# The first two weight groups of a stage as one pair: context products of all four tiles, then the latent ones

## Chip, cores and metric

The kernel runs on one core of a Trainium2 chip. The metric is device time in microseconds of one execution, as the median of several. The time before is 1759.61 us, the median of 3 runs (1754.5 to 1765.26).

## What is computed

Two layers of a backbone over 256 latent and 256 context tokens with 1024 channels. The context tokens use the same weights. Of the second layer only the latent output is wanted, but its scans start from the context's final state, so its mixer still projects the context.

```python
for l in range(DEPTH):                       # DEPTH = 2
    need_ctx = l < DEPTH - 1
    ...
    hl = rms_norm(xl, g_pre_mix[l]) * (1.0 + ml[1]) + ml[0]
    hc = rms_norm(xc, g_pre_mix[l]) * (1.0 + mc[1]) + mc[0]
    yc, yl = mixer(hc, hl, lp, lb_all[l], rows, need_ctx)
    xl = xl + ml[2] * rms_norm(yl, g_post_mix[l])
    hl = rms_norm(xl, g_pre_ffn[l]) * (1.0 + ml[4]) + ml[3]
    xl = xl + ml[5] * rms_norm(conv_ffn(hl, ffn_w_up[l], ...), g_post_ffn[l])
    if need_ctx:
        ...                                  # the same for xc
```

The mixer begins with `z = h @ w_in` (the first 1024 columns feed a depthwise convolution and the recurrent gates), the feed-forward stage with `u = h @ w_up`, whose 2 x 2816 columns are a gate half with a convolution and a value half that is multiplied by it.

## The kernel before

**Columns.** The activations stand as columns: `h` is a pair of tiles `hi` and `lo`, for each of eight k (128 channels each) with the latent tokens in columns 0 to 255 and the context tokens in 256 to 511. In a mixer a third block of 256 columns holds the latent tokens in column-major order, copied there by `columns_order` (L457 to L462, eight copies of `hi` and eight of `lo` on ScalarE).

**Products.** All large products run in split form. A weight group of 1024 x 256 is loaded by one transfer (`prep`, L247 to L251, tile `raw`), cut into two tiles of 128 columns, and each is split in `piece` (L224 to L238) into `whi` (ScalarE, L236) and `wlo` (VectorE, L237). `mm3` (L240 to L244) issues three products for each k: `whi` with `hi` (L242), `whi` with `lo` (L243), `wlo` with `hi` (L244). A tile over all eight k is 24 products, into one PSUM bank of the four named `mm`. `feat_group` (L253 to L263) does this for the two tiles of a group, over a list of views: one view is a slice of PSUM columns and of `h`.

**The split view.** Where a stage's `h` becomes ready in two parts, its first groups use two views, first the context columns 256 to 511, then the latent ones. A tile is then 24 context products and 24 latent products of 256 columns. That is so for the first two groups of layer two's mixer (the string PAT, L680, with `split` for n < 2), and for the first gate group and the first value group of the first layer's feed-forward stage (`ffn`, L1103 to L1109).

**What comes ahead of them.** The sub-layer before ends in `post` (from L473): for the context rows first and then the latent rows, ScalarE squares (L481), VectorE scales by the gate (L482) and adds the residual (L485), the row is squared again (L427) and scaled (L430), TensorE transposes it (L444, tiles `ax`), ScalarE writes `hi` (L449), VectorE writes `hf` (L451) and `lo` (L453). The context's `h` is so ready some time ahead of the latent one.

**What sets the order.** The program is recorded in the order of the code; a scheduler then places each instruction on its engine by priority and by when its tiles can have memory. `post` is recorded with a priority offset of 3000 and the splitting of weights with one of 300. Each engine runs its list in that order. Pieces come from the pool `wp` with three buffers of `whi` and of `wlo`; `raw` has three buffers too. A pool opened for a stage (`rg` in the mixer, `fw` in the feed-forward stage) lies where the pool `xp` of the rows lay before, and its tiles wait for the last use of what was there. Between the groups `aside` (L266) issues steps of the next conditioning vectors, whose additions are L306 and L308 on VectorE.

**After the second place.** The evacuation of a tile of the first 1024 columns is `conv` (ScalarE L555, VectorE L559). With two tiles done, `recur` issues eight gate products (L605), whose results ScalarE turns into sigmoids (L93) after a table load.

```python
    def feat_group(self, w, c0, views, evac, pieces=None):
        narrow = all(sl.stop - sl.start < 512 for sl, _ in views)
        pieces = pieces or self.prep(w, c0, line=int(narrow))
        for mt, (hi, lo) in enumerate(pieces):
            ps = self.psum()
            for sl, mv in views:
                for k in range(KD):
                    self.mm3(ps[:, sl], (hi[:, k, :], lo[:, k, :]), mv(k), k == 0, k == KD - 1)
            evac(c0 // P + mt, ps)
        self.aside()
```

Of the kernel before, what the change touches and what calls it, by code (L numbers as in the profile page):

```python
# [14 lines left out]
P = 128  # L15
D = 1024
KD = D // P
S = 256
DEPTH = 2
DFF = 2816  # L20
# [11 lines left out]
PAT = ['XFRXFRXFRXFFRFFF', 'XXRXFRXFRFFFRFFF']  # L32
# [19 lines left out]
class Net:  # L52
# [200 lines left out]
# [7 lines that stand above are left out]
                for k in range(KD):  # L260
                    self.mm3(ps[:, sl], (hi[:, k, :], lo[:, k, :]), mv(k), k == 0, k == KD - 1)
            evac(c0 // P + mt, ps)
        self.aside()  # L263


# [268 lines left out]
    def rg_phase(self, l, h, need_ctx, dr, first, more):  # L534
        nc, tc, I = self.nc, self.tc, self.ins
        C = self.cols[l]
        w_in = I["w_in"][l]
# [6 lines left out]
        with tc.tile_pool(name=self.nm("rg"), bufs=1, reuse_waits="tile") as pool:  # L544
# [106 lines left out]
            rgx = [(O_RGX + g * 256, conv) for g in range(4)]  # L651

            split = [(slice(S, 512), lambda k: (h[0][:, k, S:512], h[1][:, k, S:512])), lat[0]]
# [12 lines left out]
            def groups(lst, n, view):  # L666
                for _ in range(n):
                    c0, ev = lst.pop(0)
                    if c0 is None:
                        spill_v(ev)  # L670
                        continue
                    if first:
                        for mt, ps in enumerate(first.pop(0)):
                            ev(c0 // P + mt, ps)
                        continue
                    self.feat_group(w_in, c0, view, ev)

            gate_w(0), gate_w(1)
            b = 0
            for n, c in enumerate(PAT[l]):  # L680
                if c == "R":
                    recur((2 * b, 2 * b + 1))
                    b += 1
                    if b == 1:
                        self.columns_order(h)
                    if b < 4:
                        gate_w(2 * b), gate_w(2 * b + 1)
                elif c == "X":
                    groups(rgx, 1, split if n < 2 else both)
                else:  # L690
                    groups(fill, 1, main if need_ctx and n > 1 or not need_ctx else split)
# [376 lines left out]
    def ffn(self, l, h, need_ctx, ffp, pool):  # L1068
# [3 lines left out]
        w = I["ffn_w_up"][l]  # L1072
        view = [(slice(0, W), lambda k: (h[0][:, k, 0:W], h[1][:, k, 0:W]))]
# [26 lines left out]
                nc.scalar.activation(out=fh[st][t], in_=fs, func=AF.Copy)  # L1100
                nc.vector.tensor_tensor(out=fl[st][t], in0=fs, in1=fh[st][t], op=ALU.subtract)

        split = view  # L1103
        if need_ctx:
            split = [(slice(S, 512), lambda k: (h[0][:, k, S:512], h[1][:, k, S:512])),
                     (slice(0, S), lambda k: (h[0][:, k, 0:S], h[1][:, k, 0:S]))]
        for g in range(KF // 2):
            self.feat_group(w, g * 256, view if g else split, gpart)
            self.feat_group(w, DFF + g * 256, view if g else split, vpart)  # L1109
        return fh, fl  # L1110

    def run(self):
# [169 lines left out]
```

## Time and profile before

| what | value |
|---|---|
| median of 3 runs | 1759.61 us (1754.5 to 1765.26) |
| the profiled execution, its own time | 1755.87 us |
| its span | 1754.1 us |
| TensorE busy in the span | 1678.9 us, 96% |
| VectorE, ScalarE, GpSimd busy | 1269.9, 903.1, 39.6 us |
| mean granted clock of TensorE | 0.993 |
| moved by DMA | 282.91 MB, mean 161 GB/s |

The span runs from the first to the last instruction of the profiled execution. Busy shares are means over stages with different limits. A row of the timeline gives start, duration, engine, line, operation, what it writes and reads, how many were merged, and in square brackets how long the engine stood idle before it and which instruction released it. Products overlap, so their durations are longer than their distance. Some product records are missing from a trace.

### The profile page before, as it was taken

Reading aid. Unit: us, or ns where it says so; the run is one execution under the profiler, and the core shown is the slowest. Engines: PE = TensorE matmul, PEld = TensorE weight load, DVE = VectorE, ACT = ScalarE, POOL = GpSimd, SP = SyncE. Lnnn points to the kernel's source line nnn. Section 1 sums busy time; section 2 is a strip of 40 time slices with the busy share of each in tenths; the row PEclk is TensorE's granted clock in tenths of the full one; section 3 lists DMA queues with packets and bytes.
Section 4 is the critical chain, followed back from the end, with each engine's and each line's share of the span. In section 5 each row is a group of like instructions: output and inputs, shape, how many; then the busy total and the mean of one; then the engine's idle time right before and its main releaser. Section 6 shows DMA issues by size and latency. Waiting matters only on the chain.

```text
span 1754.1 us, 30468 instructions
## 1 busy us (share of the span) xinstructions
PE 1678.9 (96%) x12243; PEld 1411.8 (80%) x12243; DVE 1269.9 (72%) x2305; ACT 903.1 (51%) x1563; POOL 39.6 (2%) x65
## 2 busy tenths in 40 slices
PE   5999999999999999999999999999999999979998
PEld 3777888888888787878878877778997778969996
DVE  3788777788697787997776466777557777767764
ACT  4887723344444445533333355888445555556543
POOL 1000000000000000000000000000000000000000
PEclk9999999999999999999999999999999999989999
DMA  9422376332333377445554575332873224555663
GB/s 299 134 84 85 125 230 220 121 121 98 98 123 100 108 252 267 149 162 195 182 194 141 192 267 194 103 96 91 268 241 126 85 85 133 161 189 193 194 226 120
DMA packets 234201, 282.91 MB, mean 161 GB/s; under 512 B 16028, under 2 KB 210236, under 8 KB 234060
## 3 DMA queue, kind: packets, MB, share of 16 engines
q1 hardware_dynamic: 231068, 271.35, 46.9%
q10 hardware_dynamic: 2880, 9.51, 1.6%
q8 instruction: 96, 1.57, 0.4%
q14 instruction: 45, 0.37, 0.1%
q0 software_dynamic: 112, 0.11, 0.0%
HBM read 263.09 MB, written 17.85 MB: 160 GB/s over the span
## 4 chain that ended last, share of the span: by engine, by line
PE 71%; DVE 14%; ACT 6%; DMA 5%; issue 2%; POOL 1%; SPq 1%; POOLq 0%; DVEq 0%; ACTq 0%
PE mm L242 17%; PE mm L243 17%; PE mm L244 17%; DVE wlo L237 3%; PE mm L514 3%; PE mm L513 3%; PE mm L516 3%; DMA raw<-in_w_ada_dram 2%; DVE acc L308 2%; ACT whi L236 2%; PE ax L858 1%; ACT r L93 1%; PE ax L514 1%; PE ax L516 1%; POOL rs L418 1%
## 5 line engine op out<-in xcount | busy, mean ns | idle before, releaser
L242 PE MATMUL mm<-hi,whi 128*128 128x512 f32 (+1 forms) x1792 | 617.9, 346 | 1.5 <-ACT whi L236 1.0
L243 PE MATMUL mm<-lo,whi 128*128 128x512 f32 (+1 forms) x1792 | 615.0, 343 | 4.3 <-DVE lo L453 4.2
L237 DVE TENSOR_TENSOR wlo<-raw,whi 128x1024 fp32r<-128x1024 f32 (+1 forms) x408 | 436.2, 1080 | 249.0 <-ACT whi L236 236.1
L244 PE MATMUL mm<-hi,wlo 128*128 128x512 f32 (+1 forms) x1792 | 613.8, 343 | 2.1 <-DVE wlo L237 2.0
L236 ACT ACTIVATE whi<-raw 128x1024 fp32r<-128x1024 f32 (+1 forms) x408 | 378.8, 944 | 444.0 <-PE mm L243 223.1
L242 PEld LDWEIGHTS mm<-hi,whi 128*128 128x128 f32 x1792 | 337.4, 189 | 46.9 <-issue 4.3
L243 PEld LDWEIGHTS mm<-lo,whi 128*128 128x128 f32 x1792 | 337.5, 188 | 45.2 <-DVE lo L453 5.6
L244 PEld LDWEIGHTS mm<-hi,wlo 128*128 128x128 f32 x1792 | 336.8, 188 | 43.0 <-DVE wlo L237 3.1
L308 DVE SCALAR_TENSOR_TENSOR acc<-raw,s,acc 128x256 f32<-128x256 f32 x448 | 192.7, 478 | 1.8
L873 DVE TENSOR_TENSOR QK<-QK,T 128x512 f32<-128x512 f32 (+1 forms) x84 | 101.6, 1220 | 9.6 <-PE ax L858 6.3
L243 PE MATMUL mm<-wlo,hi 128*128 128x256 f32 x256 | 71.4, 279 | 3.1 <-DVE wlo L237 3.1
L242 PE MATMUL mm<-whi,hi 128*128 128x256 f32 x256 | 72.1, 282 | 1.1 <-ACT whi L236 0.9
L882 ACT ACTIVATE kt<-QK 128x256 f32<-128x256 f32 (+1 forms) x60 | 40.9, 690 | 58.8 <-DVE QK L873 38.3
L244 PE MATMUL mm<-whi,lo 128*128 128x256 f32 x256 | 71.2, 278 | 0.0
L514 PE MATMUL mm<-wlo,fh 128*128 128x512 f32 x176 | 68.5, 389 | 0.0
L513 PE MATMUL mm<-whi,fh 128*128 128x512 f32 x176 | 68.5, 389 | 0.0
L418 POOL TENSOR_TENSOR rs<-ms,mhalf 128x1 f32<-128x1 f32 (+2 forms) x42 | 29.4, 701 | 1535.4 <-DVE ms L416 1535.4
L516 PE MATMUL mm<-whi,fl 128*128 128x512 f32 x176 | 54.2, 389 | 0.0
L243 PEld LDWEIGHTS mm<-wlo,hi 128*128 128x128 f32 x256 | 48.1, 188 | 3.8 <-DVE wlo L237 3.5
L242 PEld LDWEIGHTS mm<-whi,hi 128*128 128x128 f32 x256 | 48.2, 188 | 3.0 <-ACT whi L236 1.1
L93 ACT ACTIVATE acc<-acc 128x512 f32<-128x512 f32 (+1 forms) x44 | 22.6, 515 | 53.9 <-DVE acc L1089 53.9
L244 PEld LDWEIGHTS mm<-whi,lo 128*128 128x128 f32 x256 | 48.3, 189 | 0.0
(225 smaller groups left out, 2456.3 us busy)
## 6 DMA issues: line engine op xcount, KB each, us to landing
raw<-in_w_in_dram SPq DMA_DIRECT2D x72, 1024.0 KB
raw<-in_w_ada_dram SPq DMA_DIRECT2D x48, 1024.0 KB
raw<-in_ffn_w_up_dram SPq DMA_DIRECT2D x44, 1024.0 KB
raw<-in_ffn_w_down_dram SPq DMA_DIRECT2D x33, 1024.0 KB
raw<-in_w_out_dram SPq DMA_DIRECT2D x12, 1024.0 KB
raw<-in_w_proj_rg_dram SPq DMA_DIRECT2D x8, 1024.0 KB
raw<-in_w_proj_hg_dram SPq DMA_DIRECT2D x8, 1024.0 KB
xs<-xt SPq DMA_DIRECT2D x10, 512.0 KB
```

The lines of the kernel that those rows point to most:

```text
L236: nc.scalar.activation(out=v(hi)[:, part, :], in_=src[:, part, :], func=AF.Copy)
L237: nc.vector.tensor_tensor(out=v(lo)[:, part, :], in0=src[:, part, :], in1=v(hi)[:, part, :], op=ALU.subtract)
L242: nc.tensor.matmul(out=out, lhsT=L[0], rhs=R[0], start=start, stop=False)
L243: nc.tensor.matmul(out=out, lhsT=L[0], rhs=R[1], start=False, stop=False)
L244: nc.tensor.matmul(out=out, lhsT=L[1], rhs=R[0], start=False, stop=stop)
L308: nc.vector.scalar_tensor_tensor(out=at, in0=r3[:, k, :], scalar=s, in1=at, op0=ALU.mult, op1=ALU.add)
L418: nc.gpsimd.tensor_tensor(out=rs, in0=ms, in1=self.mhalf[:, 0:n], op=ALU.pow)
L513: nc.tensor.matmul(out=out, lhsT=ah, rhs=hi[:, n, :], start=k == 0, stop=False)
L514: nc.tensor.matmul(out=out, lhsT=ah, rhs=lo[:, n, :], start=False, stop=False)
L516: nc.tensor.matmul(out=pss[i][n], lhsT=al, rhs=hi[:, n, :], start=False, stop=k == nk - 1)
L873: nc.vector.tensor_tensor(out=u, in0=u, in1=sub(t, 1, [[-1, 2], [2, W2 // B], [0, B]]), op=ALU.mult)
L882: nc.scalar.activation(out=kt.rearrange("p (n h j) -> p n h j", h=2, j=B), in_=sub(qk, W2, [[2 * B, W2 // (2 * B)], [W2 + B, 2], [1, B]]), ...
```

## The change

A new function `feat_pair` takes two groups. It splits the first group's tiles into the pool `wp` as before and the second group's tiles into the pool of the stage, takes four PSUM banks, issues the context products of all four tiles, then the latent products of all four, then the four evacuations. It replaces the first two groups of layer two's mixer, and the first gate and value group of the first layer's feed-forward stage.

```diff
+    def feat_pair(self, parts, views, pool):
+        jobs = []
+        for j, (w, c0, evac) in enumerate(parts):
+            for mt, p in enumerate(self.prep(w, c0, (pool, pool) if j else (None, None), 1)):
+                jobs.append((c0 // P + mt, p, evac, self.psum()))
+        for sl, mv in views:
+            for _, (hi, lo), _, ps in jobs:
+                for k in range(KD):
+                    self.mm3(ps[:, sl], (hi[:, k, :], lo[:, k, :]), mv(k), k == 0, k == KD - 1)
+        for m, _, evac, ps in jobs:
+            evac(m, ps)
+        self.aside()
+        self.aside()
...
-            for n, c in enumerate(PAT[l]):
+            pat = PAT[l]
+            if not need_ctx:
+                assert pat[:2] == "XX"
+                self.feat_pair([(w_in, *rgx.pop(0)) for _ in range(2)], split, pool)
+                pat = "  " + pat[2:]
+            for n, c in enumerate(pat):
+                if c == " ":
+                    continue
...
         for g in range(KF // 2):
-            self.feat_group(w, g * 256, view if g else split, gpart)
-            self.feat_group(w, DFF + g * 256, view if g else split, vpart)
+            if need_ctx and not g:
+                self.feat_pair([(w, 0, gpart), (w, DFF, vpart)], split, pool)
+                continue
+            self.feat_group(w, g * 256, view, gpart)
+            self.feat_group(w, DFF + g * 256, view, vpart)
```

The lines behind `feat_group` are numbered 15 higher after the change (L444 is L459 there, and so on). Below, tiles have their running numbers.

**TensorE, first feed-forward stage, at the last transposes of the latent rows.** Before, mm_7053 and mm_7109 are tiles one and two, mm_7187 is tile three:

```order
L444 MATMUL ax_6921<-ident_99,xh_6834 128x128
L444 MATMUL ax_6921<-ident_99,xh_6835 128x128
L242 MATMUL mm_7053<-hi_6439,whi_7033 128x256
L242 MATMUL mm_7109<-hi_6439,whi_7043 128x256
L244 MATMUL mm_7187<-hi_6439,wlo_7168 128x256
L242 MATMUL mm_7187<-hi_6439,whi_7167 128x256
L243 MATMUL mm_7187<-lo_6440,whi_7167 128x256
```

After, mm_7053 and mm_7054 are tiles one and two:

```order
L459 MATMUL ax_6921<-ident_99,xh_6834 128x128
L459 MATMUL ax_6921<-ident_99,xh_6835 128x128
L242 MATMUL mm_7053<-hi_6439,whi_7033 128x256
L242 MATMUL mm_7054<-hi_6439,whi_7043 128x256
L351 MATMUL ax_7295<-ident_99,row_6412 128x128
L382 MATMUL ax_7299<-acc_6416,ones_584 32x128 x4
L243 MATMUL mm_7053<-lo_6440,whi_7033 128x256
```

Of tile three 17 products stood ahead of these transposes, 8 right behind them, and 8 more between the latent products of k 0 to 3 and those of k 4 to 7 of tiles one and two. None stands there now: the first product of tile three (mm_7077) comes after 22 of the 24 latent products of tile one.

**TensorE, layer two, at the second half of the latent columns.** Before, mm_10134 and mm_10188 are tiles one and two, mm_10264 is tile three, and the last three rows are the second half of tile one:

```order
L244 MATMUL mm_10264<-hi_9504,wlo_10245 128x256
L242 MATMUL mm_10264<-hi_9504,whi_10244 128x256
L243 MATMUL mm_10134<-lo_9505,whi_10114 128x256
L244 MATMUL mm_10134<-hi_9504,wlo_10115 128x256
L242 MATMUL mm_10134<-hi_9504,whi_10114 128x256
```

After, tile one's tenth product of that half is followed by the first ones of tiles three and four (mm_10158, mm_10159):

```order
L242 MATMUL mm_10134<-hi_9504,whi_10114 128x256
L243 MATMUL mm_10134<-lo_9505,whi_10114 128x256
L242 MATMUL mm_10158<-hi_9504,whi_10138 128x256
L243 MATMUL mm_10158<-lo_9505,whi_10138 128x256
L244 MATMUL mm_10134<-hi_9504,wlo_10115 128x256
L242 MATMUL mm_10159<-hi_9504,whi_10148 128x256
L244 MATMUL mm_10158<-hi_9504,wlo_10139 128x256
```

Before, 13 products of tile three stood ahead of the last transposes, 12 behind them and 6 ahead of the second half; 87 products followed from there to the gate products. Now none of tile three or four stands ahead of it. Eleven products of tile two's second half stand behind the context products of tiles three and four.

**ScalarE, layer two, behind the norm.** Before, all eight column copies of the low part, then the pieces of tile four; tile three's four pieces stood ahead of the squares of the last latent row:

```order
L449 ACTIVATE hi_9504<-ax_10084,mc_1777,acol_1778 128x256
L460 ACTIVATE lo_9505<-lo_9505 128x256
L460 ACTIVATE hi_9504<-hi_9504 128x256 x4
L460 ACTIVATE lo_9505<-lo_9505 128x256 x4
L236 ACTIVATE whi_10254<-raw_10242 128x256 x4
L555 ACTIVATE xg_10183<-mm_10134,cols_835,cols_825 128x512
```

After, the pieces of tiles three and four in turn, with two of the column copies behind them:

```order
L464 ACTIVATE hi_9504<-ax_10084,mc_1777,acol_1778 128x256
L475 ACTIVATE lo_9505<-lo_9505 128x256
L475 ACTIVATE hi_9504<-hi_9504 128x256 x4
L475 ACTIVATE lo_9505<-lo_9505 128x256 x2
L236 ACTIVATE whi_10138<-raw_10136 128x256
L236 ACTIVATE whi_10148<-raw_10136 128x256
```

Tile three's place ahead of the last latent row's squares is taken by four pieces of the next group. In the feed-forward stage the pieces of tiles three and four stand in the same way behind the last latent `hi`, and on VectorE behind the last latent `lo` and two pieces of the next group.

## Rows read from the trace of the kernel before

**Rows 1.** The page: busy time, granted clock by slice, chain by engine.

```profile
PE 1678.9 (96%) x12243; PEld 1411.8 (80%) x12243; DVE 1269.9 (72%) x2305; ACT 903.1 (51%) x1563; POOL 39.6 (2%) x65
...
PEclk9999999999999999999999999999999999989999
...
PE 71%; DVE 14%; ACT 6%; DMA 5%; issue 2%; POOL 1%; SPq 1%; POOLq 0%; DVEq 0%; ACTq 0%
```

**Rows 2.** Waits of TensorE, 1110 to 1754 us: total, times, longest.

```profile
PE mm L243 <- DVE wlo L237: 3.1, 2, 2.0
...
PE ax L605 <- ACT q L93: 2.3, 2, 1.2
```

**Rows 3.** Timeline of TensorE, first feed-forward stage (start, duration, ..., idle before).

```profile
710.01 0.39 PE L244 MATMUL mm<-hi,wlo 128*128 128x256 f32 x1 [1.40 <-DVE wlo L237]
712.36 1.53 PE L444 MATMUL ax<-ident,xh 128*128 128x128 f32 x12 [0.37 <-DVE xh L430]
716.06 0.30 PE L336 MATMUL ax<-ident,row 128*128 128x128 f32 x1 [1.02 <-DVE hf L451]
...
720.54 0.28 PE L242 MATMUL mm<-hi,whi 128*128 128x256 f32 x1
720.66 0.28 PE L243 MATMUL mm<-lo,whi 128*128 128x256 f32 x1
...
730.90 0.39 PE L242 MATMUL mm<-hi,whi 128*128 128x512 f32 x1
```

**Rows 4.** Timeline of VectorE, first feed-forward stage.

```profile
712.88 0.88 DVE L308 SCALAR_TENSOR_TENSOR acc<-raw,s,acc 128x256 f32<-128x256 f32 x2
...
719.76 1.28 DVE L453 TENSOR_TENSOR lo<-hf,hi 128x512 fp32r<-128x512 f32 x2
...
722.72 1.43 DVE L237 TENSOR_TENSOR wlo<-raw,whi 128x256 fp32r<-128x256 f32 x4
```

**Rows 5.** Timeline of TensorE, entry of layer two.

```profile
1091.09 1.09 PE L444 MATMUL ax<-ident,xh 128*128 128x128 f32 x8 [1.48 <-DVE xh L430]
...
1095.29 0.39 PE L243 MATMUL mm<-lo,whi 128*128 128x256 f32 x1 [1.07 <-DVE lo L453]
...
1100.54 0.38 PE L243 MATMUL mm<-lo,whi 128*128 128x256 f32 x1 [1.55 <-DVE lo L453]
...
1111.18 3.67 PE L605 MATMUL ax<-xg,gwr 128*128 128x512 f32 x8
...
1117.96 0.79 PE L243 MATMUL mm<-lo,whi 128*128 128x512 f32 x1
```

**Rows 6.** Timeline of ScalarE, entry of layer two.

```profile
1101.95 2.35 ACT L460 ACTIVATE lo<-lo 128x256 fp32r<-128x256 f32 x4
1104.19 1.34 ACT L236 ACTIVATE whi<-raw 128x256 fp32r<-128x256 f32 x4
...
1111.93 0.76 ACT L555 ACTIVATE xg<-mm,cols,cols 128x512 f32<-128x512 f32 x1
1112.71 1.28 ACT L93 ACT_TABLE_LOAD   x1
1114.01 0.69 ACT L93 ACTIVATE r<-ax,cols 128x512 f32<-128x512 f32 x1
```

**Rows 7.** Stretches of 4 us: length, busy of each engine (instructions), granted clock, DMA.

```profile
1484.00:1488.00 4.00, 1.33 (x21) 1.03 (x21) 3.10 (x9) 3.35 (x10) 0.00 (x0) 1.00 0.15 31
1488.00:1492.00 4.00, 4.00 (x22) 4.00 (x22) 1.26 (x6) 1.64 (x5) 0.00 (x0) 0.57 0.67 231
...
1564.00:1568.00 4.00, 3.42 (x22) 3.13 (x21) 3.64 (x7) 3.04 (x7) 0.00 (x0) 0.66 0.06 24
1568.00:1572.00 4.00, 4.00 (x38) 4.00 (x37) 3.02 (x6) 0.80 (x3) 0.00 (x0) 1.00 0.00 0
```

**Rows 8.** Timeline of TensorE, entry of the last feed-forward stage.

```profile
1557.11 1.08 PE L444 MATMUL ax<-ident,xh 128*128 128x128 f32 x4 [3.83 <-DVE xh L430]
1562.69 2.82 PE L444 MATMUL ax<-ident,xh 128*128 128x128 f32 x12 [4.49 <-DVE xh L430]
```

More of the change, by code (lines that the diff above doesn't have):

```diff
@@ L1101, in vpart @@
                 nc.vector.tensor_tensor(out=fl[st][t], in0=fs, in1=fh[st][t], op=ALU.subtract)
-        split = view
         if need_ctx:
```

## The prediction

> **What bounds the kernel now.** I read the page first. TensorE is busy for 1678.9 of 1754.1 us, 96%, at full clock in nearly every slice, and it holds 71% of the chain that ended last [rows 1]. So time goes wherever TensorE stands still, and an edit that neither adds nor removes a product can only move that standing. Next comes the list of what TensorE waited for in the second layer, which shows that waits are few there and come from chains on ScalarE and VectorE [rows 2]. The change touches two places of the same kind, so I read the timeline of each: the last token rows of the sub-layer before are normalised on ScalarE and VectorE, and TensorE meanwhile runs the context parts of the next sub-layer, because the context columns were ready earlier.
>
> At the first place (entry of the first feed-forward stage) TensorE finishes the context parts of tiles one and two by 708.6 us, stands still for 1.40 us, runs context products of tile three, transposes at 712.36, and waits 1.02 us more [rows 3]. From there to the first 512-wide product at 730.90 it hardly stops. The second half of the latent columns comes from the two subtractions that begin at 719.76 and last 1.28 us [rows 4].
>
> At the second place (entry of layer two) the waits that the view names are 1.48, 1.07 and 1.55 us [rows 5]. All of them are for the norm chain. Both chains end long after the context work runs out, so the amount of ready context work decides how long TensorE stands.
>
> **The change part by part.** No product, piece or transfer is added or removed. What moves is the order, and the order shown above is not what the diff suggests. The pieces of the second group now come from the stage's own pool. In the order of ScalarE they stand behind the latent columns of the norm (first place) and behind six of the eight copies of the low part (second place), while before, tile three was split before the norm ended. So TensorE has two context parts ahead of the norm, not four, and not three as before.
>
> *First place, lost cover.* Before, 25 products of tile three (2 among the first transposes, 15 before the last twelve, 8 behind them) ran ahead of the first latent product that needs a low part, and 8 of its latent products between the two halves. These 33 now come later. One product costs 0.12 us by its neighbours' starts, 720.54 and 720.66; over longer stretches 0.115, which I use [rows 3]. 33 x 0.115 = **+3.8 us**, all of it on the path, since the norm chain sets when the latent products begin.
>
> *First place, VectorE relieved.* Between the last row scaling and the last latent low part VectorE ran six additions for the conditioning at 0.44 us (0.88 for two), 2.6 us. In the new order it runs three of them and one piece of 0.36 (1.43 for four) [rows 4], 1.7 us. **-0.9 us**.
>
> *First place, the pair's own pieces.* They end ten pieces of 0.36 us after the last low part, 3.6 us. TensorE has 33 products, 3.8 us, to run before it needs the last one. Zero, and the cover is thin: a VectorE that is 1 us late would cost that 1 us. The place gives +2.9.
>
> *Second place, lost cover.* 13 products of tile three before the last transposes, 12 behind them and 6 before the second half: 31 x 0.115 = **+3.6 us**.
>
> *Second place, the pair's pieces.* TensorE starts on the second half at 1100.54 [rows 5] and has ten products to run, until 1101.7. ScalarE starts the four copies of the low part at 1101.95 and takes 2.35 us for them [rows 6]. Two of them now stand ahead of the first piece, so it starts at 1103.1, takes about 0.4 us (1.34 for four, overlapped), and is there at 1103.5: **+1.8 us** of new wait. Queued behind the waiting product are eleven ready products of tile two; they do not pass it. That order holds is seen in the same trace: eight gate products start at 1111.18, the fifth waits for the first sigmoid of 1114.01, and the second 512-wide product, which waited for nothing, starts only at 1117.96 [rows 5, 6].
>
> *Second place, end.* Before, 87 products from 1100.54 would have ended at 1110.55, and the gate products began at 1111.18: 0.6 us of slack goes. Then the eight gate products: before, the fifth could start when the first sigmoid ended, 1114.01 + 0.69, 3.5 us after the first. Now the last convolution (0.76), the table load (1.28) and the first sigmoid (0.69) [rows 6] with some 0.3 to start follow the last product, 3.0 us. 0.6 + 0.5, **-1.1 us** together. The place gives +4.3.
>
> *The clock.* Waits of up to 1.55 us at the second place left the slice of the page at 9 [rows 1]. The new waits are longer: before the last transposes of the first place 1.40 + 0.37 us and the 17 products between and ahead of them, 3.7 us in one piece. The nearest rows are the two waits at the entry of the last feed-forward stage, 3.83 and 4.49 us, behind which twelve transposes took 2.82 us instead of 1.53 [rows 3, 8] and the granted clock of the next 4 us was 0.66, so the level of 1.2 GHz for part of them and 2.4 GHz after [rows 7]. A fall costs 1.3 us on those transposes and, by 22 instructions in 4 us instead of 38 in the next 4 [rows 7], at most 1.1 more when the 0.58 us that TensorE was not busy is taken off. Ends 0 and 2.4; I take one fall at the first place, at **+1.5**, since its gap is nearest to the 3.83 that fell. The Trainium skill (TensorE: Matmul & The Clock Gate, section "A second HAM failure mode: psum-queue depth-cycling") has the clock swing between its two levels also where TensorE stands only briefly but often; by that the second place falls as well, and the sum would be 1.5 higher. The rows of before show three waits in a row there, each up to 1.55 us, in a slice of full clock, which does not bear it out for waits of that size.
>
> *Further on.* VectorE's share of the gate chain starts some 2.7 us later instead of 4.3, since the convolutions of tiles one to three are done earlier relative to the gates. The two waits for split weights, 3.1 us together [rows 2], hang on that chain: between 0 and 1.6 us come back, I take **-0.7**.
>
> Sum: 2.9 + 4.3 + 1.5 - 0.7 = **+8.0 us**. The profiled execution took 1755.87 us (span 1754.1), which gives 1763.9. It lies 3.7 us under the median of the runs shown, 1759.61, so I carry the shift to the median: **1767.6 us**, 0.45% more. What a measurement of this kernel can tell from no change is about 0.5%, 8.8 us. The forecast is a loss that stays just under it.
>
> **The rivals.** *The clock falls at both places.* With their lost cover the waits of the second place become 1.48 + 1.5 = 3.0 us before the last transposes, 1.07 + 1.4 = 2.5 before the first latent low part, 1.55 + 0.7 = 2.2 before the second half, and 1.8 for the piece. If the clock falls in them too, each place costs up to 2.4: 2.9 + 4.3 + 4.8 = +12.0, 1771.6 us, slower. For it: at 1488 to 1492 us the clock stood at 0.57 after a stretch of 4 us in which TensorE was busy for 1.33, not still [rows 7]. Against it: the three waits there left no trace in the clock before [rows 1, 5]. It decides if any wait of the second place is followed by a granted clock below 1.
>
> *The change does what it says.* If the context parts of all four tiles did run inside the norm's waits, tile four's 24 products (2.8 us) would fill waits of 2.8 us at the first place and 4.1 at the second [rows 3, 5]: -5.6 us, 1754.0 us, not slower. The listed order speaks against it: the second pair's pieces and products stand behind the norm. It would need the pieces to be written before the last transposes.
>
> *The loss is swallowed.* The gate chain of layer two is long on ScalarE and VectorE, and TensorE waits 2.3 us for its sigmoids and 3.1 us for weights split behind it [rows 2]. If that chain, not TensorE, sets the end of the stage and starts hardly later, 4 us of the second place come back and no clock falls: +3 us, 1762.6. Against it: the first sigmoid itself stands behind the last convolution and so behind the last product.
>
> **How the numbers follow.** Forecast 0.66, with +5 to +12 as its own spread; clock at both places 0.16; swallowed 0.12; change works as named 0.06. Over 8.8 us lie a good third of the forecast (0.24) and nearly all of the clock case: slower 0.40. Faster by more than 8.8 us is out of reach of every mechanism here, since the waits of both places hold only 6.9 us; 0.03 for a scatter of the runs. Same 0.57. The range goes from 1758 (the low end of the swallowed case counted from the profiled execution, +2) to 1776 (the clock case with its waits all at the high end and the runs' scatter of 5 us above the median).
>
> **What would show it.** In the timeline of the first place: products of tiles one and two end near 708.4, nothing until the transposes near 712.4, the first product of the pair's second group after 721, the first 512-wide product at 733 to 736 instead of 730.90. At the second place: a wait of some 1.8 us for a piece split on line 236 near 1102 to 1104 (times of before, plus the shift of the first place), and the gate products 4 to 7 us later than 1111.18 after that shift is taken off. The granted clock near 712 to 718 shows whether it fell. The prediction is wrong if the second group's pieces are written before the last transposes, if the shift at either place has the other sign, or if the stage that follows gives back more than 2 us.

## The result and the profile after

The changed kernel takes **1769.77 us** (median of 17 runs, 1763.16 to 1773.65) beside 1756.82 us of the kernel before on the same chip (17 runs, 1751.84 to 1765.26): a ratio of 1.0068, 95% interval [1.0055, 1.0081], 12 us more (10 to 14); the two medians themselves lie 12.95 us apart. A second comparison on another occasion gave 1.0067 [1.0048, 1.0085]. The forecast was 1767.6 us in a range from 1758 to 1776, +8.0 us by its sum. Sign and range were right, the size was four microseconds short. That the forecast's time lies only 2.2 us under the measured one is in part luck: its base, the median of three runs, lay 2.8 us above the median of 17 found here. By the prediction's own line of 8.8 us a loss of 12 us is "slower", to which it gave 0.40, and not "same", to which it gave 0.57. The profiled execution took 1764.91 us (span 1763.1), 9.0 us more than the profiled one before; it is the second shortest of the 17.

The page of the changed kernel, answering to [rows 1]. TensorE is busy for 6.8 us more with the same 12243 products, which says little by itself (a second profile of the kernel before has 1689.7 us), and one more slice of the granted clock drops to 8:

```profile
PE 1685.7 (96%) x12243; PEld 1417.4 (80%) x12243; DVE 1271.8 (72%) x2305; ACT 904.3 (51%) x1563; POOL 39.8 (2%) x65
...
PEclk9999999999999999899999999999999999989999
...
PE 69%; DVE 14%; ACT 6%; DMA 6%; issue 2%; POOL 1%; SPq 1%; DVEq 0%; POOLq 0%; ACTq 0%
```

The first place (entry of the first feed-forward stage), timeline of TensorE: start, duration, line, work, and in brackets the idle time before. All lines lie 15 further down than before where they stand behind the new function. It answers to [rows 3]:

```profile
702.40 0.28 PE L242 MATMUL mm<-hi,whi 128*128 128x256 f32 x1
...
707.45 0.83 PE L459 MATMUL ax<-ident,xh 128*128 128x128 f32 x4
713.28 2.82 PE L459 MATMUL ax<-ident,xh 128*128 128x128 f32 x12 [3.84 <-DVE xh L445]
717.25 0.45 PE L351 MATMUL ax<-ident,row 128*128 128x128 f32 x1 [0.72 <-DVE hf L466]
...
736.27 0.40 PE L242 MATMUL mm<-hi,whi 128*128 128x512 f32 x1
```

One wait of 3.84 us stands where there were two of 1.40 and 0.37, and the last twelve transposes take 2.82 us instead of 1.53. To compare executions that start at different times, I count from the first context product of the place, 702.40 here and 701.58 before, to the first 512-wide product: 33.87 us here, 29.32 before.

The second place (entry of layer two), answering to [rows 5]:

```profile
1085.86 0.28 PE L242 MATMUL mm<-hi,whi 128*128 128x256 f32 x1
...
1096.25 1.96 PE L459 MATMUL ax<-ident,xh 128*128 128x128 f32 x12 [3.24 <-DVE xh L445]
1100.45 0.58 PE L243 MATMUL mm<-lo,whi 128*128 128x256 f32 x1 [1.82 <-DVE lo L468]
1105.63 0.38 PE L243 MATMUL mm<-lo,whi 128*128 128x256 f32 x1 [0.51 <-DVE lo L468]
1108.58 0.39 PE L242 MATMUL mm<-hi,whi 128*128 128x256 f32 x1 [1.53 <-ACT whi L236]
1121.16 7.03 PE L620 MATMUL ax<-xg,gwr 128*128 128x512 f32 x16
```

Here is the new wait of 1.53 us for a piece of the second group. ScalarE, answering to [rows 6], shows why: two copies of the low part stand ahead of the pieces, and two behind them.

```profile
1107.01 1.22 ACT L475 ACTIVATE lo<-lo 128x256 fp32r<-128x256 f32 x2
1108.06 3.83 ACT L236 ACTIVATE whi<-raw 128x256 fp32r<-128x256 f32 x12
1111.75 0.81 ACT L570 ACTIVATE xg<-mm,cols,cols 128x512 f32<-128x512 f32 x1
1112.41 1.29 ACT L475 ACTIVATE lo<-lo 128x256 fp32r<-128x256 f32 x2
```

From the first context product of this place (1080.71 before) to the gate products it is 35.30 us, and 30.47 before. Stretches of 4 us show the clock, columns as in [rows 7]. The kernel before, one stretch of the first place and one of the second:

```profile
712.00:716.00 4.00, 2.68 (x22) 2.48 (x22) 4.00 (x11) 2.84 (x6) 0.00 (x0) 1.00 0.46 175
...
1096.00:1100.00 4.00, 2.99 (x27) 2.79 (x25) 1.86 (x5) 4.00 (x9) 0.00 (x0) 1.00 0.04 9
```

The changed kernel, the first place and then the second:

```profile
708.00:712.00 4.00, 1.44 (x10) 1.04 (x9) 3.56 (x12) 1.40 (x4) 0.59 (x1) 0.94 0.54 177
712.00:716.00 4.00, 2.72 (x13) 2.72 (x14) 3.06 (x8) 1.62 (x4) 0.66 (x1) 0.50 0.61 220
716.00:720.00 4.00, 3.28 (x20) 2.36 (x20) 3.84 (x10) 3.57 (x11) 0.00 (x0) 0.50 0.00 0
720.00:724.00 4.00, 4.00 (x29) 4.00 (x29) 4.00 (x10) 2.71 (x9) 0.00 (x0) 0.78 0.00 0
...
1094.00:1098.00 4.00, 1.75 (x13) 1.76 (x13) 2.42 (x6) 1.17 (x3) 1.48 (x3) 0.90 0.74 252
1098.00:1102.00 4.00, 2.18 (x10) 1.89 (x10) 3.54 (x7) 4.00 (x9) 0.00 (x0) 0.50 0.22 49
1102.00:1106.00 4.00, 3.49 (x22) 3.29 (x22) 2.02 (x4) 4.00 (x9) 0.00 (x0) 0.75 0.00 0
1106.00:1110.00 4.00, 2.47 (x22) 2.27 (x21) 1.61 (x6) 4.00 (x12) 0.00 (x0) 1.00 0.00 0
```

TensorE goes down to half level (0.50, which is 1.2 GHz) at **both** places; I call such a stretch a fall. Before, the clock stood at 1.00 in every 4 us stretch of both. The page does not show the second one: a slice of it is 44 us long, and there it reads 9 after the change as before it.

The span divides at these places. Its 9.0 us are 0.82 ahead of the first place, 4.33 from there to the second, 3.86 from there to the last feed-forward stage's first transposes (1557.11 before, 1566.12 after), and nothing from there on (197.0 us both times).

### The profile page after: what moved, and what is told of

It reads as the page before. It is cut to its first block, busy times and chain, and to the rows that moved or that the text cites. A ratio compares the mean times of both kernels' runs of the same rounds, so it can differ in the third digit from the quotient of the medians.

```text
span 1763.1 us, 30467 instructions
## 1 busy us (share of the span) xinstructions
PE 1685.7 (96%) x12243; PEld 1417.4 (80%) x12243; DVE 1271.8 (72%) x2305; ACT 904.3 (51%) x1563; POOL 39.8 (2%) x65
## 4 chain that ended last, share of the span: by engine, by line
PE 69%; DVE 14%; ACT 6%; DMA 6%; issue 2%; POOL 1%; SPq 1%; DVEq 0%; POOLq 0%; ACTq 0%
PE mm L242 17%; PE mm L243 17%; PE mm L244 16%; DVE wlo L237 3%; PE mm L529 3%; PE mm L528 3%; PE mm L531 3%; DMA raw<-in_w_ada_dram 2%; ACT whi L236 2%; DVE acc L323 1%; PE ax L880 1%; ACT r L93 1%; PE ax L529 1%; PE ax L531 1%; POOL rs L433 1%
```

## Experiments

All ratios are to the kernel before on the same chip. Two numbers are read from every profile: *place one*, from its first context product to the first 512-wide product, and *place two*, from its first context product to the gate products. They are left out for the first group split alone, where other products lie in these stretches.

| kernel | place one, us | place two, us | ratio, 95% interval |
|---|---|---|---|
| before / before again | 29.32 / 28.81 | 30.47 / 30.50 | 1.0001 [0.9984, 1.0018] (again) |
| the change | 33.87 | 35.30 | 1.0068 [1.0055, 1.0081] |
| the change again / a third profile | 32.87 / 33.23 | 35.50 / 36.03 | 1.0067 [1.0048, 1.0085] (again) |
| pair in the feed-forward stage alone | 32.62 | 30.48 | 1.0025 [1.0007, 1.0042] |
| pair in the mixer alone | 28.82 | 35.44 | 1.0026 [1.0006, 1.0045] |
| 24 products repeated | 32.14 | 37.43 | 1.0053 [1.0032, 1.0074] |
| 48 products repeated | 32.14 | 38.61 | 1.0085 [1.0063, 1.0108] |
| tile three's pieces early | 28.79 | 31.95 | 1.0001 [0.9986, 1.0017] |
| first group split alone | | | 1.0030 [1.0013, 1.0048] |
| four buffers, pair | 27.57 | 30.84 | 1.0302 [1.0283, 1.0322] |
| four buffers, no pair | 27.58 | 30.92 | 1.0281 [1.0263, 1.0299] |
| last entry filled | 28.79 | 30.46 | 0.9987 [0.9972, 1.0001] |

### The change in halves

First the mixer goes back to the order before:

```diff
@@ mixer of layer two
-            if not need_ctx:
+            if False:
                 assert pat[:2] == "XX"
                 self.feat_pair([(w_in, *rgx.pop(0)) for _ in range(2)], split, pool)
```

> The pair is kept in the first feed-forward stage alone; the mixer of layer two is as before the change. Theory A (each place loses the cover of tile three's context products and, on top, the clock falls there): this place's share alone, +4.5 us against the kernel before (+3 to +6), granted clock near 0.5 for some 8 to 10 us behind the last twelve transposes of this place, and the entry of layer two as before, with no fall there. Rival B (the clock's falls, not the cover, are the loss, and one place's fall makes the other's more likely): the two places singly give clearly less than the whole change together, +2 us or less each. Rival C (the loss is made at the second place and further on alone, as the first is hidden by what follows): 0 to +1 us.

Measured: +4.4 us (1.2 to 7.4), with place one at 32.62 us and place two as before. Then the feed-forward stage goes back:

```diff
@@ first feed-forward stage
-            if need_ctx and not g:
-                self.feat_pair([(w, 0, gpart), (w, DFF, vpart)], split, pool)
-                continue
+            v = split if need_ctx and not g else view
-            self.feat_group(w, g * 256, view, gpart)
-            self.feat_group(w, DFF + g * 256, view, vpart)
+            self.feat_group(w, g * 256, v, gpart)
+            self.feat_group(w, DFF + g * 256, v, vpart)
```

> The pair is kept in the mixer of layer two alone; the first feed-forward stage is as before the change. Theory A (lost cover and a fall of the clock at each place): +5 us against the kernel before (+3.5 to +7), granted clock near 0.5 for some 6 us at the entry of layer two, 1.00 at the first place. Together with the run that has the pair in the feed-forward stage alone it sums to the whole change's +9 to +12. Rival B (falls depend on each other): +2 us or less, clock at or near 1.00 here. Rival C (all of the loss is here): +9 us or more.

Measured: +4.6 us (1.1 to 7.9), place two at 35.44 us and place one as before. Each place carries its own loss; the two sum to +9.0 where the whole measured +12. C falls by the intervals. B doesn't, since its 2 us lie inside both; it falls by the places, which are 3.3 and 5.0 us longer than in the first profile before. One part of A was off: in the first half the clock was down for less time than the 8 to 10 us expected. Stretches of the kernel with the pair in the feed-forward stage alone, place one:

```profile
716.00:720.00 4.00, 2.07 (x11) 2.07 (x12) 3.31 (x11) 1.23 (x3) 0.66 (x1) 0.78 0.79 287
720.00:724.00 4.00, 3.05 (x25) 2.36 (x24) 3.84 (x9) 3.57 (x10) 0.00 (x0) 0.79 0.00 0
724.00:728.00 4.00, 3.86 (x33) 3.62 (x32) 4.00 (x11) 3.21 (x11) 0.00 (x0) 1.00 0.00 0
```

Averages of 0.78 and 0.79 over 4 us each are some 3.4 us at half level; the change's own 0.94, 0.50, 0.50 and 0.78 are some 10 us. The instructions of this place are the same in both.

### The cover given back

Tile three takes its pieces from the third buffer again, tile four from the stage's pool:

```diff
-            for mt, p in enumerate(self.prep(w, c0, (pool, pool) if j else (None, None), 1)):
+            for mt, p in enumerate(self.prep(w, c0, (None, pool) if j else (None, None), 1)):
```

> The changed kernel, but the first tile of the second group (tile three) takes its pieces from the third buffer of the weights' pool, as it did before the change; tile four still takes them from the stage's pool. Theory A (what was lost is tile three's context cover): three context parts run ahead of the norm again, the clock stays at 1.00 at the first place, and the time is that of the kernel before, within -1 to +3 us. Rival F (the order of the pair itself, all context parts and then all latent parts, or the pieces from the stage's pool, cost the time, and not tile three's cover): half or more of the loss stays, +5 us or more.

Measured: ratio 1.0001, that is +0.2 us (-2.5 to +3.0). TensorE's timeline of this kernel at place one, and its wait for the piece at place two:

```profile
711.84 1.42 PE L459 MATMUL ax<-ident,xh 128*128 128x128 f32 x11 [0.37 <-DVE xh L445]
...
729.87 0.40 PE L242 MATMUL mm<-hi,whi 128*128 128x512 f32 x1
...
1103.52 0.38 PE L242 MATMUL mm<-hi,whi 128*128 128x256 f32 x1 [1.49 <-ACT whi L236]
```

The wait before the transposes is 0.37 us as before, they take their full speed, and place one is as quick as before. Place two keeps some 1.5 us: tile four's pieces still come from the stage's pool, and the wait for them is still there. One word, a pool's name, undoes the rest of the loss. (That the pool's tiles come late because they wait for the memory under them is read from the code; no run tests it apart from the pool.)

The other way round: the kernel before with only its first group split, so that two context parts stand ahead of the norm and nothing else of the change is there.

```diff
-                    groups(rgx, 1, split if n < 2 else both)
+                    groups(rgx, 1, split if n < 1 else both)
@@ first feed-forward stage
             self.feat_group(w, g * 256, view if g else split, gpart)
-            self.feat_group(w, DFF + g * 256, view if g else split, vpart)
+            self.feat_group(w, DFF + g * 256, view, vpart)
```

> The kernel before, with only the first group of each of the two stages split into context and latent part; the second group runs whole behind the norm. No pair, no pieces from the stage's pool. So two context parts stand ahead of the norm, as in the changed kernel, and nothing else of the change is there. Theory A (the loss is the cover of tile three, with the clock's fall in the longer wait): at the first place as the changed kernel, +3 to +5 us, with the wait before the last twelve transposes at 3.8 us; at the second +3 to +4, as the wait for a piece of the second group (1.5 us) is not there; in all +6 to +9 us against the kernel before. Rival F (pair order or pieces from the stage's pool make the loss): 0 to +2 us.

Measured: +5.3 us (2.3 to 8.4), a little under A's span, with an interval that reaches into it, and above F's. TensorE's timeline shows the change's two waits, and the clock's fall in the length of the transposes, without any pair:

```profile
710.82 2.82 PE L444 MATMUL ax<-ident,xh 128*128 128x128 f32 x12 [3.74 <-DVE xh L430]
...
1095.19 2.77 PE L444 MATMUL ax<-ident,xh 128*128 128x128 f32 x12 [3.23 <-DVE xh L430]
```

### The order of the pair by itself

A fourth buffer in the weights' pool lets all pieces come early; room for it comes from the raw weights, and from 16 unused elements of each piece's row (not listed). A control has the same buffers and no pair.

```diff
-        return pool.tile([P, 2048], F32, tag="raw", name=self.nm("raw"), bufs=3)
+        return pool.tile([P, 2048], F32, tag="raw", name=self.nm("raw"), bufs=2)
@@ piece
-        pool, bufs = (pool, 2) if pool else (self.wp, 3)
+        pool, bufs = (pool, 2) if pool else (self.wp, 4)
...
@@ feat_pair (not in the control)
-            for mt, p in enumerate(self.prep(w, c0, (pool, pool) if j else (None, None), 1)):
+            for mt, p in enumerate(self.prep(w, c0, (None, None), 1)):
```

> The changed kernel with all four tiles' pieces from the weights' pool, which gets a fourth buffer of each kind (the raw weights get two buffers instead of three, and the pieces' rows lose 16 unused elements, to make room). By the listed order tile three's context part and 4 products of tile four's run ahead of the last transposes of the first place. Theory A (what counts is how many context products stand ahead of the norm): the first place is at least as quick as before, 28.3 to 29.3 us from its first context product to the first 512-wide one (29.3 before, 33.9 after), no fall of the clock; in all -1 to +1 us against the control with the same buffers. Rival F (the order of the pair costs): +3 us or more against that control.

> The kernel before with the same buffers as the run with four buffers (four of each kind of piece, two of raw weights, 16 unused elements less), and no pair: the control for that run. The third raw buffer may have hidden some loads; expected 0 to +4 us against the kernel before, at the two places as before.

Measured: 1811.3 and 1808.2 us, ratios 1.0302 and 1.0281, intervals that overlap. The 3.1 us between the medians are as much as F asked for, but four runs each don't tell them from nothing. The places decide: 27.57 and 27.58 us, 30.84 and 30.92 us. (Of the 8.7 us between the two profiled spans 8.4 lie ahead of the first place, where the code is the same.) TensorE's timeline, place one of the kernel with four buffers and the pair:

```profile
730.09 0.28 PE L242 MATMUL mm<-hi,whi 128*128 128x256 f32 x1
...
757.66 0.50 PE L242 MATMUL mm<-hi,whi 128*128 128x512 f32 x1
```

and of its control:

```profile
721.71 0.28 PE L242 MATMUL mm<-hi,whi 128*128 128x256 f32 x1
...
749.29 0.50 PE L242 MATMUL mm<-hi,whi 128*128 128x512 f32 x1
```

So "all context parts, then all latent parts" costs nothing where the pieces are there in time, and gains nothing measurable there either. F falls by the places. The control's own price was a miss: +49 us where 0 to 4 were expected. With two raw buffers the loads come late, ScalarE's split of the weights waits for them and TensorE for the split; before, TensorE's wait was 2.0 us in all and ScalarE's 7.8. That is a part of the 49 us; where the rest lies is not shown. The lists of waits of the control, of TensorE and of ScalarE (total, times, longest):

```profile
PE mm L242 <- ACT whi L236: 15.0, 13, 5.5
```

```profile
ACT whi L236 <- DMA raw<-in_w_out_dram: 30.8, 8, 8.3
```

### The clock by itself

The changed kernel with the 24 context products of tile two, and then those of tiles one and two, issued twice:

```diff
-        for sl, mv in views:
-            for _, (hi, lo), _, ps in jobs:
-                for k in range(KD):
+        for v, (sl, mv) in enumerate(views):
+            for i, (_, (hi, lo), _, ps) in enumerate(jobs):
+                for k in list(range(KD)) * (2 if v == 0 and i == 1 else 1):
```

(with `i < 2` for the 48)

> The changed kernel with the 24 context products of tile two issued twice at both places: the second set writes the same sums again and only fills the time in which TensorE stood still for the norm. The lost cover stays as it is. Theory A with the clock as a part of the loss: granted clock stays at or near 1.00 at both places, the last twelve transposes take 1.5 us instead of 2.8, and 2 to 3 us come back per place: +4 to +7 us against the kernel before, where the change has +9 to +12. Rival D (the clock's fall costs nothing, since the products that run slowly there wait for the norm's columns anyway): the same as the change, +9 to +12, although the clock stays up. Rival E (the repeated products are in the way of the transposes): above +13.

> The changed kernel with the context products of both tiles of the first group issued twice (48 more at each place, 5.5 us of TensorE time, into waits of 3.8 and 3.2 us and what follows them). The sums are written again with the same values. Theory A: no fall of the clock at either place; the first place costs what the 24 repeats left of it plus what of the other 24 does not fit, 32.5 to 34 us; the second has its gate products at 36 to 38 us, since the repeats that do not fit push all that follows. It tells whether the fall of the clock at the second place cost anything: if it did, the gate products come earlier than 35.3 us in spite of the repeats.

Measured: +9.3 us (5.6 to 13.0) and +15.0 us (11.1 to 19.0). At place one the clock does what A said: granted clock 1.00 throughout, transposes in 1.53 us, 32.14 us both times. That is 0.5 to 1.7 us less than in the four profiles with a fall, so a fall there costs something, against D, but less than A's 2 to 3. At place two the clock falls all the same. Stretches of the kernel with 24 repeats, place two:

```profile
1094.00:1098.00 4.00, 2.82 (x24) 2.62 (x23) 2.93 (x6) 4.00 (x9) 0.00 (x0) 1.00 0.19 43
1098.00:1102.00 4.00, 1.83 (x15) 1.63 (x14) 2.20 (x4) 4.00 (x9) 0.00 (x0) 0.97 0.00 0
1102.00:1106.00 4.00, 2.69 (x13) 2.40 (x13) 2.38 (x8) 4.00 (x13) 0.00 (x0) 0.50 0.00 0
1106.00:1110.00 4.00, 4.00 (x26) 4.00 (x26) 3.90 (x9) 2.71 (x7) 0.00 (x0) 0.67 0.61 195
```

The fall is not gone, it comes later: waits of 1.83, 1.18, 2.17 and 1.31 us are left, and half level now lies on the run of ready products behind them, where nothing covers it: 37.43 us instead of 35.30 to 36.03. The repeats are not in the way: TensorE starts on the second half of the latent columns 19.84 us into the place, with the same 118 products to run to the gate products as in the changed kernel, and takes 17.59 us for them instead of 15.53. So this fall costs 2.1 us. What one place gave back the other took, and the total could not tell A from D; the two places could. With 48 repeats the same fall stands at place two (0.50 from 1102 to 1106 us), and nine repeated products more behind it.

The same question in the kernel before, at the entry of the last feed-forward stage [rows 8]: 14 products of a piece with itself in the first wait and 36 repeated transposes in the second.

```diff
...
             ps = self.psum()
+            for i in range(filler if not mt else 0):
+                k = i % KD
+                self.nc.tensor.matmul(out=ps, lhsT=hi[:, k, :], rhs=hi[:, 4 * (k // 4):4 * (k // 4) + 4, :], start=True, stop=True)
@@ norm_cols
+        for _ in range(self.again):
+            nc.tensor.transpose(p3[:, 0, 0:P], xh[0][:, 2 * k2 * P:(2 * k2 + 1) * P], self.ident)
...
```

(`filler` is 14 for the first gate group of that stage and 0 elsewhere, `again` is 9 for the rows ahead of it and 0 elsewhere.)

> The kernel before, with TensorE kept running at the entry of the last feed-forward stage, where it stood 3.83 and 4.49 us and the clock fell: 14 products of a piece with itself, 512 wide, into the sum that the first real product starts anew, and 36 repeats of the first half's transposes, also overwritten. They compute nothing new. It measures the price of one fall by itself. Theory A: the clock stays at 1.00 there, the last twelve transposes take 1.5 us instead of 2.82, and 1.3 to 2.4 us come back in that stretch, -1 to -2.5 us in all. Rival D (what runs slowly there waits for the norm's columns anyway, so a fall costs nothing): transposes shorter, 0 to -0.5 us in all. Rival E (the repeats are in the way of the transposes): slower.

Measured: -2.3 us (-4.9 to +0.2), not told apart from no change. In the profile the clock stayed at 1.00 through the transposes, but the first latent low part came no sooner (14.2 us after the start of the last two products ahead of the entry, 14.1 before). Stretches of this kernel:

```profile
1560.00:1564.00 4.00, 2.10 (x17) 1.90 (x17) 2.23 (x5) 2.31 (x6) 0.52 (x1) 1.00 0.58 215
1564.00:1568.00 4.00, 2.69 (x12) 2.70 (x13) 3.82 (x9) 1.55 (x4) 0.00 (x0) 0.67 0.00 0
```

TensorE then waited 2.10 us for VectorE's subtraction, which now stood behind four `hf` steps, not three, and the fall again came later, on ready products. The run has two edits in one, quicker transposes and another order on VectorE, so it prices neither.

### The change again, and the kernel before against itself

> The changed kernel once more, beside the kernel before on the same chip. The two places measured in the profiles are 4.55 and 4.8 us longer than before, and the two halves of the change measured singly sum to +9.0 us, while the first comparison of the whole gave +12. If the halves add up, +9 to +10 us here too; if the whole is more than its halves, +12. In the profile, if the time that TensorE stays at half its clock varies from execution to execution: the first place anywhere from 32.2 to 33.9 us from its first context product to the first 512-wide one; if it belongs to the code: 33.9 us again.

> The changed kernel a third time, one look: the same question of the clock. If the fall's length varies from execution to execution, a length other than the 10 us at half level that the first profile had at the first place, and a first place of 32.2 to 33.9 us; the second place's gate products at 35.3 us after its first context product, whatever the clock does there, since its columns set the pace.

> The kernel before against itself: what the comparison shows where nothing is changed, and a second profile of it. Expected: a ratio within 0.9985 to 1.0015. In the profile, the first place 28.8 to 29.4 us from its first context product to the first 512-wide one, the second with its gate products at 30.5 us, 476.4 us from the second place to the first transposes of the last feed-forward stage, and from there to the end 197.0 or 201.2 us, the two lengths that the profiles of other versions had with the same products at the same granted clock.

Measured: ratio 1.0067 [1.0048, 1.0085] for the change, 1.0001 [0.9984, 1.0018] for the kernel before, and 1768.33 us for the single execution. Place one is 32.87 and 33.23 us: with the first profile and the half-change, four executions of the same instructions give 32.62 to 33.87. The fall is there each time and its length is not the code's. The expectation that place two keeps 35.3 us whatever the clock does was wrong in the third profile: its transposes took 2.82 us and its gate products stood at 36.03. The second profile before has 28.81 us at place one, as have, within 0.02 us, the three others in which tile three covers the wait; the 29.32 of the first profile is the odd one.

## Why the prediction held, point by point

- **The order.** Right. The second group's pieces came behind the norm at both places, so two context parts stood ahead of it. Giving tile three its buffer back took the loss away (1.0001); taking its split away made it without the pair (1.0030).
- **Place one, lost cover +3.8, VectorE -0.9, pieces 0: +2.9.** The sum is right, one term of it is not. Without a fall of the clock place one is 32.14 us, 2.8 above the one profile before and 3.3 above the other. From the first product that needs a low part to the first 512-wide one the run with 24 repeats takes 17.06 us, against 13.88 and 13.37 before: the lost cover is 3.2 to 3.7, as forecast. But VectorE's relief is about half of its term. The two steps for the latent low parts begin 14.34 and 17.68 us into the place there, and 14.70 and 18.18 before: 0.4 and 0.5 us earlier. And where the clock falls they come later than before, 15.07 and 18.42 us into the place in the first profile of the change, since VectorE then waits for ScalarE, which follows the slower transposes. VectorE's rows, of the kernel before, with 24 repeats (the place begins at 699.03 us there), and of the change:

```profile
716.28 1.28 DVE L453 TENSOR_TENSOR lo<-hf,hi 128x512 fp32r<-128x512 f32 x2
```

```profile
713.37 1.28 DVE L468 TENSOR_TENSOR lo<-hf,hi 128x512 fp32r<-128x512 f32 x2
```

```profile
714.82 1.19 DVE L466 TENSOR_SCALAR hf<-ax,acol,mc 128x256 f32<-128x256 f32 x2 [0.41 <-ACT hi L464]
...
717.47 1.28 DVE L468 TENSOR_TENSOR lo<-hf,hi 128x512 fp32r<-128x512 f32 x2
```

The 0 for the pair's pieces holds: no wait for them appears.

- **Place two, lost cover +3.6, pieces +1.8, slack -0.6: +4.8 up to the gate products.** Right: +4.8, +5.0 and +5.6 in the three profiles, and +5.0 in the mixer alone. The wait for the piece is 1.51 to 1.53 us in all of them, 0.3 less than forecast.
- **End of the gates -0.5, further on -0.7.** From the second place's start to the last feed-forward stage the forecast was 4.3 - 0.7 = +3.6 us. Three of four profiles give +3.6 to +3.9 over the first profile before, the third profile of the change +6.0. The second profile before is itself 1.75 us above the first there, so the two terms are not told apart, and -0.7 is not shown by itself.
- **The clock, "one fall at the first place, at +1.5".** Here the step failed. The first place's price is 0.5 to 1.7 us over 32.14 in four executions, so 1.5 was a fair size; but the sentence "which does not bear it out for waits of that size" closed the second place, and the clock fell there in every profile of the change. The sentence is true of waits of 1.48, 1.07 and 1.55 us: the clock stood at 1.00 behind them in both profiles before. But the change makes them longer, by the prediction's own rival 3.0 us before the transposes, and 3.24 were measured. That was the first rival's condition. The Trainium skill (TensorE: Matmul & The Clock Gate, section "A second HAM failure mode: psum-queue depth-cycling") has the clock swing also where TensorE stands briefly but often; the run with 24 repeats agrees, 0.50 from 1102 to 1106 us with waits of 1.83, 1.18, 2.17 and 1.31 around it, while the kernel before and the run with tile three's pieces early (1.07, 1.46 and 1.49 us, clock 1.00) don't show it. The rival's price at the second place, up to 2.4 us, is not in the profiles of the change: TensorE reached the second half of the latent columns 19.77 us into the place in the first profile, and 19.83 before, so half level lay under waits for the norm and cost nothing there; in the mixer alone and in the second profile it cost 0.1 and 0.2, in the third 0.7, as the transposes were slower.
- **The sum.** Means over the profiles: the stretch from place one to place two is 382.95 us with the pair in the first (four) and 379.33 without (three), +3.6; from place two to the last feed-forward stage 480.68 (four) and 477.13 (three), +3.5. Together +7.2 where the forecast has +8.0. The comparisons of all runs say +12, with 10 to 14 in the first and 8 to 15 in the second. That is the sum of the first rival, +12.0; its terms are not what the profiles show.

**What stays open** is that gap of some 4 us. The stretches differ by up to 2.3 us between profiles of the same code, and the halves of the change sum to +9.0, so a part of the gap may be chance. The profiled executions of the change are short ones, the second shortest of 17 and the shortest of 6; the third profile, nearer to the median, has +10.3 in the two stretches against the first profile before. In the second comparison the six runs go from 1765.17 us at a mean granted clock of 0.992 to 1776.01 at 0.987, and the change's mean over these runs is 0.989, that of the kernel before 0.993. That points to falls that last longer in most executions than in the profiled ones. But in the first comparison time and clock are unrelated: the mean clock of its 17 runs is 0.989, which is also that of the profiled one, 4.9 us under their median. So it is not shown.

Of the other rivals, "the change does what it says" fell with the listed order, and "the loss is swallowed" (+3 in all) with the measured +12 (10 to 14); of place two's +5.0 the stretch up to the last feed-forward stage keeps +3.5, where this rival gives 4 back. No version tried is faster than the kernel before beyond its interval.

## What to carry to other kernels

Before counting what a reordering covers, ask where the operands of the moved work are written: here another pool put a group's weights behind the wait that they were to cover, and the order of products was of no matter. Price a fall of the clock by what lies under it: half level under a wait cost 0 to 0.7 us here, on some 5 us of ready products it cost 2.1, and filling a part of the wait may only move the fall onto those. Where the whole differs by half a per cent, read the stretches between fixed points of the trace; totals of single executions differ by more than the effect.

## What the runs showed that I had not expected

**Two rates of the same products at the same granted clock.** In the feed-forward stage of layer two, stretches of 40 us of the kernel before, in its first profile and in its second:

```profile
1600.00:1640.00 40.00, 40.00 (x355) 40.00 (x354) 29.17 (x43) 23.59 (x37) 0.00 (x0) 1.00 0.60 194
```

```profile
1600.00:1640.00 40.00, 40.00 (x342) 40.00 (x342) 29.17 (x44) 22.61 (x36) 0.00 (x0) 1.00 0.56 185
```

One code, one granted clock, 0.113 and 0.117 us a product. From the last entry to the end this is 197.0 or 201.2 us in most profiles, whatever the kernel (203.1 in this second one): a scatter of 4 us that belongs to the execution. At the first place it was the other way round: the first profile took 13.88 us for the latent products up to the first 512-wide one, the second 13.37. What sets the rate was not found. The start of place one also scatters, from 697.7 to 707.0 us behind the same instructions.

**The length of a fall.** The same instructions at place one had the clock down for some 3.4 us in three executions and 10 us in one, at a price of 0.5 to 1.1 us and of 1.7.
